# Projections of the linear attention and of the spatial gating given as units between the steps of the long convolutions

## The chip, the core and the metric

The kernel runs on one core of a Trainium2 chip. A core has five engines with a queue each: TensorE (PE; matmuls, with weight loads shown apart as PEld), VectorE (DVE), ScalarE (ACT), GpSimd (POOL) and SyncE (SP), which issues all DMA transfers of this kernel. The metric is the device time of one execution in microseconds (us).

## The reference, cut to what matters

One trunk layer is computed for 256 context tokens and 1024 latent tokens of width 1024. The input is normalised and modulated to `h`; one projection feeds four token mixers side by side, whose outputs are merged by `w_out`; a SwiGLU feed-forward block follows.

```python
h = rmsnorm(x, lp['g_pre1']) * (1.0 + sc1) + sh1
p = h @ lp['w_in']
ya = short_conv_mixer(p[..., :o1], lp['conv_a'], row_w)
yb, s_new = gla_mixer(p[..., o1:o2], s0, ...)       # linear attention
yc = chunk_mlp_mixer(p[..., o2:o3], ...)            # spatial gating
yd = hyena_mixer(p[..., o3:], ...)                  # long convolutions
m = jnp.concatenate([ya, yb, yc, yd], axis=-1) @ lp['w_out']
```

The long convolutions (`hyena_mixer`) gate a sequence twice with a bidirectional convolution as long as the sequence, by Fourier transforms. They need only their own columns of `p`. The linear attention needs its queries, keys, values, gates and decays, the spatial gating its two halves, all of them further columns of `p`.

## The kernel before

Everything is float32, and each product is made of three matmuls of split operands (`mm3`, lines 90 to 92): a high part and a remainder of each side. `hh` and `hl` hold the two parts of the transposed `h` for three column blocks of 512, 512 and 256 tokens (`CH`). `load_split` loads a weight (SyncE), casts it to its high part (ScalarE, line 65) and subtracts for the remainder (mostly DVE, line 66), in the seven tiles of pool `s4`.

A projection is cut into units. `proj_fm` makes 128 feature rows for one block: 24 matmuls of 512 or 256 columns into a PSUM bank (`pg`, four of them). `proj_rows` does so for three blocks, copies each with an activation on ScalarE and stores it to DRAM: three units to a weight. `proj_b` makes the linear attention's projections: gate rows with two weights (lines 866 and 867, six units) and then ten token tiles of 128 tokens by 288 columns (values and decays, 24 matmuls each; line 881 transposes the decays, line 883 copies them). `proj_c` makes the spatial gating's: two weights of feature rows (six units, copies on line 766) and ten token tiles of 256 columns (copies on line 778). These are 16 units each. `proj_c` is the beginning of the generator `fillers`, which goes on with the short convolutions (`mixer_a`) and the first tiles of `w_out`. `load_w` also steps the generator `later`, which loads the remaining modulation weights piece by piece and multiplies them (line 164).

`mixer_d` makes the long convolutions in 16 steps: two convolutions (`o`) of two channel tiles (`ct`), two halves (`q`) and two frequency tiles (`ft`). A step has a front (`hyena_front`: six matmuls of 320 columns from tiles `zh` and `zl` into a bank `p`, then scaling on ScalarE, lines 729 to 732, and combination on DVE, line 733, to a tile `Y`), and a back (`hyena_back`: butterflies and the product with the filter's spectrum `kk`, lines 705 to 751, on DVE, POOL and ScalarE). After every second step an inverse (`hyena_inverse`: twelve matmuls of 320 columns from `yh` and `yl`, lines 696 to 699) gives a half of the result. The back of a step is written behind the front of the next. At the end the results are transposed (lines 662 and 669), copied (665, 671, 672) and stored.

In `run`, `mixer_d` stands whole, then `proj_b` whole, then 17 steps of `fillers` (the 16 units of `proj_c` and the first of `mixer_a`), then `mixer_b`, the linear attention, which takes further units of `fillers` at marked places. The queries and keys are projected inside `mixer_b` by `proj_rows`.

The order of the code is not the order on the engines. The layer that builds the program puts the instructions on each engine's queue by priority, earlier code first, among those that it expects to be ready at that point, with tiles, banks and semaphores to be had. An engine then executes its queue in order. `tc.high_priority` and `tc.issue_after` bend that order in a few places.

Of the kernel before, what the change touches and what calls it, by code (L numbers as in the profile page):

```python
# [13 lines left out]
AF = mybir.ActivationFunctionType  # L14
# [4 lines left out]
P = 128  # L19
# [22 lines left out]
class Builder:  # L42
# [193 lines left out]
    def run(self):  # L236
        tc, nc, a = self.tc, self.nc, self.a
        with ExitStack() as ctx:
# [83 lines left out]
                    self.filter_spectra(flk, h2)  # L322
            rows = self.proj_d(w)
            with tc.tile_pool(name="psd", bufs=2, space=PSUM, reuse_waits="tile") as psd, sub("dm", side="right") as dm:
                self.mixer_d(dm, psd)
            self.proj_b(rows)
            self.wo, self.act1 = {}, (self.hh, self.hl)
            fill = self.fillers()
            for _ in range(17):
                next(fill)  # L330
            with banks() as self.psm, sub("bm", side="right") as bmx:
                self.mixer_b(bmx, fill)
            for _ in fill:
# [287 lines left out]
        xg = self.xg[kind][ct]  # L621
        nc.sync.dma_start(xg[:, n, 0:4, :] if n < 2 else xg[:, :, 4, :], sg[:, :N].rearrange("p (d c) -> p d c", c=P))

    def mixer_d(self, dm, psd):
        nc = self.nc
        self.p2 = lambda: psd.tile([P, 2, 512], F32, tag="p2", name=self.nm("p2"))
        self.hyena_consts(dm)
        zs = []
        for ct in range(2):
            z = dm.tile([P, 2, 5, P], F32, tag="z", bufs=3, name=self.nm("z"))  # L630
            nc.sync.dma_start(z, self.xg[0][ct])
            zs.append(z)
        back, done = None, []
        for o in range(2):
            for ct in range(2):
                z, gate = zs[ct], dm.tile([P, 2, 5, P], F32, tag="gate", bufs=1, name=self.nm("gate"))
                nc.sync.dma_start(gate, self.xg[o + 1][ct])
                zs[ct] = dm.tile([P, 2, 5, P], F32, tag="z", bufs=3, name=self.nm("z"))
                for q in (slice(0, 64), slice(64, 128)):
                    zq = self.hyena_split(dm, z[:, :, :, q])  # L640
                    ys = []
                    for ft in range(2):
                        kk = dm.tile([P, 5, 2, 64], F32, tag="kk", bufs=3, name=self.nm("kk"))
                        nc.sync.dma_start(kk, self.kd[o][ft][:, ct, :, :, q])
                        X = self.hyena_front(dm, ft, *zq)
                        if done:
                            self.hyena_inverse(dm, *done.pop())
                        if back:
                            back()

                        def back(X=X, ft=ft, ys=ys, kk=kk, gate=gate[:, :, :, q], dst=zs[ct][:, :, :, q]):
                            ys.append(self.hyena_back(dm, X, kk, ft))
                            if ft:
                                done.append((ys, gate, dst))
        back()
        self.hyena_inverse(dm, *done.pop())
        for ct in range(2):
            y2 = zs[ct]
            for kt in range(2):
                pt = self.p2()[:, 0]  # L660
                for p in range(4):
                    nc.tensor.transpose(pt[:, p * P:(p + 1) * P], y2[:, kt, p, :], self.ident)
                sg = dm.tile([P, 512], F32, tag="W", bufs=2, name=self.nm("dy"))
                pv = pt.rearrange("c (p u) -> c p u", p=4)
                nc.scalar.copy(sg.rearrange("c (u p) -> c p u", p=4), pv[:, :, ::-1] if kt else pv)
                nc.sync.dma_start(self.yd[6 + ct][:, kt * 512:(kt + 1) * 512], sg)
            pt = self.p2()[:, 0]
            for kt in range(2):
                nc.tensor.transpose(pt[:, kt * P:(kt + 1) * P], y2[:, kt, 4, :], self.ident)
            sg = dm.tile([P, 512], F32, tag="W", bufs=2, name=self.nm("dy"))  # L670
            nc.scalar.copy(sg[:, :P], pt[:, :P])
            nc.scalar.copy(sg[:, P:256], pt[:, 255:127:-1])
            nc.sync.dma_start(self.yd[6 + ct][:, 1024:1280], sg[:, :256])
# [46 lines left out]
    def hyena_front(self, dm, ft, zh, zl):  # L720

        nc = self.nc
        X = dm.tile([P, 5, 2, 64], F32, tag="Y", bufs=5, name=self.nm("Y"))
        t = dm.tile([P, 3, 2, 64], F32, tag="dt", bufs=2, name=self.nm("dt"))
        ps = self.p2()[:, :, :320].rearrange("p r (a c) -> p r a c", c=64)
        for ri in range(2):
            m = ri ^ ft
            self.mm3(ps[:, ri], self.dh[:, 0, ri, ft], self.dl[:, 0, ri, ft], zh[:, m], zl[:, m], True, True)
        nc.scalar.copy(X[:, ::4].rearrange("p a r c -> p r a c"), ps[:, :, ::4])
        for d in range(1, 4):  # L730
            nc.scalar.mul(t[:, d - 1, 0], ps[:, 1, d], self.twist(ft, d, 2))
            nc.scalar.mul(t[:, d - 1, 1], ps[:, 0, d], self.twist(ft, d, 1))
            nc.vector.scalar_tensor_tensor(X[:, d], ps[:, :, d], self.twist(ft, d, 0), t[:, d - 1], ALU.mult, ALU.add)
        return X

# [126 lines left out]

    def proj_b(self, rows):
        nc, a = self.nc, self.a
        self.proj_rows(rows, self.gd[0], AF.Silu)
        self.proj_rows(self.load_w(11), self.gd[1], AF.Silu)
        wv = []
        for k0, k1 in ((0, 3), (3, 6), (6, 8)):
            wv.append(self.load_split(a["wvg"][:, k0:k1, :].rearrange("p k c -> p (k c)"), (k1 - k0) * 288))
        for n, (n0, N) in enumerate(CH):  # L870
            pt = self.pg()
            for t in range(N // P):
                ps = self.pg()
                for kt in range(KT):
                    wh, wl = (x[:, (kt % 3) * 288:(kt % 3 + 1) * 288] for x in wv[kt // 3])
                    tk = slice(t * P, (t + 1) * P)
                    self.mm3(ps[:, :288], self.hh[n][:, kt, tk], self.hl[n][:, kt, tk], wh, wl, kt == 0, kt == KT - 1)
                o = self.pj()
                nc.scalar.copy(o[:, :288], ps[:, :288])
                nc.sync.dma_start(self.vd[:, n0 // P + t, :], o[:, :256])  # L880
                nc.tensor.transpose(pt[:, t * P:(t + 1) * P], o[:, 160:288], self.ident)
            o = self.pj()
            nc.scalar.copy(o[:, :N], pt[:, :N])
            nc.sync.dma_start(self.gkd[:, n0:n0 + N], o[:, :N])

    def proj_rows(self, w, dst, func, scale=1.0):
        nc = self.nc
        for n, (n0, N) in enumerate(CH):
            ps = self.proj_fm(w, n)
            o = self.pj()  # L890
            nc.scalar.activation(o[:, :N], ps[:, :N], func, scale=scale)
            nc.sync.dma_start(dst[:, n0:n0 + N], o[:, :N])

    def mixer_b(self, bm, fill):
        nc, a = self.nc, self.a
# [54 lines left out]
        cb = [x.rearrange("p (c t) -> p c t", t=P) for x in b]  # L950
        last = [cb[0][:, :, P - 1:P], cb[1][:, :, 0:1]]

        self.proj_rows(self.load_w(8), self.qd, AF.Identity, 32.0 ** -0.5)
        self.proj_rows(self.load_w(9), self.kkd, AF.Identity)

        def update(n, d):

# [51 lines left out]
        N, levels = 256, LEVELS + [0]  # L1009
# [760 lines left out]
```

## Time and profile before

| | |
|---|---|
| time, median of 3 runs | 1596.38 us (1595.15 to 1596.7) |
| profiled execution: time / span | 1599.48 us / 1597.70 us |
| mean granted TensorE clock | 0.976 of full speed |
| busy over the span: PE, PEld, DVE, ACT, POOL | 94%, 78%, 64%, 42%, 25% |
| instructions | 23281 |

The profile is of one execution. A busy figure is the time in which the engine had an instruction of its own running; matmuls are pipelined, so that a PE that is busy throughout may still run slower than it can, and the distance between the starts of two matmuls tells more than the length of one. Idle time is put down to the semaphore event that ended it.

### The profile page before, as it was taken

The numbers are of one execution on the slowest core, as the hardware profiler recorded it, in microseconds if no ns is written. First come the engines' busy times: TensorE is split into PE (matmuls) and PEld (weight loads), VectorE is DVE, ScalarE is ACT, GpSimd is POOL, SyncE is SP. The second block draws the span as 40 slices with busy tenths as digits, with TensorE's granted clock in tenths as the row PEclk, the third lists the DMA queues.
The fourth block names the chain that finished last, engine by engine and source line by source line (L and its number), as shares of the span: only waits on it lengthen the run. The fifth ranks groups of instructions, "written<-read, shape, count | busy, mean of one in ns | idle before, by whom it ended". The sixth has DMA issues, their size and how long they took to land.

```text
span 1597.7 us, 23281 instructions
## 1 busy us (share of the span) xinstructions
PE 1500.9 (94%) x8517; PEld 1239.1 (78%) x8517; DVE 1027.7 (64%) x1752; ACT 666.6 (42%) x1218; POOL 405.0 (25%) x406
## 2 busy tenths in 40 slices
PE   5999997888989889999899999999999999999996
PEld 2688877778668667788688888888888887888885
DVE  6776559999277898546746555665565635544467
ACT  5754245454356767555522222222222214433352
POOL 1433216556124665533211010101101000000004
PEclk9899999999999999999899999999999999999998
DMA  9335473442723074561134334443343428755576
GB/s 330 130 117 163 133 225 84 137 141 71 259 98 101 29 254 139 179 217 53 60 117 137 111 119 149 128 140 117 113 144 126 150 89 257 237 172 178 164 247 250
DMA packets 163226, 242.17 MB, mean 152 GB/s; under 512 B 34613, under 2 KB 97407, under 8 KB 162984
## 3 DMA queue, kind: packets, MB, share of 16 engines
q1 hardware_dynamic: 163112, 240.69, 46.2%
q8 instruction: 67, 1.10, 0.3%
q14 instruction: 47, 0.39, 0.1%
HBM read 169.05 MB, written 71.58 MB: 151 GB/s over the span
## 4 chain that ended last, share of the span: by engine, by line
PE 57%; DVE 8%; issue 3%; ACT 3%; DMA 2%; POOL 2%; SPq 0%; POOLq 0%; DVEq 0%; ACTq 0%
PE pg L1386 17%; PE pm L1386 7%; PE pg L1548 7%; PE pm L1548 6%; PE pg L92 4%; PE pg L90 4%; PE pg L91 3%; PE pm L90 3%; PE pm L92 3%; PE pm L91 3%; DMA raw<-w2t 1%; DVE qbd L1036 1%; POOL rs L98 1%; DVE hl L66 1%; PE pm L1049 1%
## 5 line engine op out<-in xcount | busy, mean ns | idle before, releaser
L92 PE MATMUL pg<-hh,s 128*128 128x512 f32 (+1 forms) x432 | 154.9, 363 | 6.7 <-DVE s L66 6.7
L90 PE MATMUL pg<-hh,s 128*128 128x512 f32 (+1 forms) x432 | 157.6, 366 | 3.7 <-ACT s L65 3.1
L66 DVE TENSOR_TENSOR op<-raw,op 128x1152 fp32r<-128x1152 f32 x69 | 93.7, 1357 | 100.6 <-ACT op L65 100.6
L91 PE MATMUL pg<-hl,s 128*128 128x512 f32 (+1 forms) x432 | 155.2, 360 | 0.6 <-POOL hl L204 0.6
L65 ACT CAST op<-raw 128x1152 fp32r<-128x1152 f32 x69 | 80.1, 1161 | 135.0 <-PE pg L1548 65.1
L1363 POOL TENSOR_TENSOR sr<-s,s 128x512 f32<-128x512 f32 x20 | 25.8, 1292 | 434.4 <-DVE sr L1361 434.4
L98 POOL TENSOR_TENSOR rs<-rs,mhalf 128x1 f32<-128x1 f32 x40 | 31.8, 798 | 354.7 <-DVE rs L97 351.4
L65 ACT CAST s<-s 128x1024 fp32r<-128x1024 f32 (+2 forms) x67 | 69.6, 1039 | 116.1 <-DMA s<-in_w 77.0
L1548 PE MATMUL pg<-op,op 128*128 128x512 f32 x372 | 115.3, 392 | 1.8 <-DVE op L66 1.8
L65 ACT CAST su<-sr 128x512 fp32r<-128x512 f32 x80 | 49.4, 620 | 149.6 <-PE pm L1386 59.7
L66 DVE TENSOR_TENSOR s<-s,s 128x1024 fp32r<-128x1024 f32 (+2 forms) x67 | 85.6, 1278 | 37.3 <-ACT s L65 20.6
L1386 PE MATMUL pg<-b1h,s 128*128 128x512 f32 x320 | 106.9, 395 | 0.7 <-ACT t L1393 0.7
L1386 PE MATMUL pg<-hh,su 128*128 128x512 f32 x320 | 107.3, 396 | 0.0
L1548 PE MATMUL pm<-op,op 128*128 128x512 f32 x338 | 104.5, 391 | 0.0
L90 PE MATMUL pm<-hh,s 128*128 128x256 f32 x352 | 100.0, 284 | 1.3 <-DVE tmp L201 1.3
L92 PE MATMUL pm<-hh,s 128*128 128x256 f32 x352 | 99.9, 284 | 0.0
L91 PE MATMUL pm<-hl,s 128*128 128x256 f32 x352 | 99.9, 284 | 0.0
L92 PEld LDWEIGHTS pg<-hh,s 128*128 128x128 f32 x432 | 82.5, 191 | 20.6 <-DVE s L66 7.6
L90 PEld LDWEIGHTS pg<-hh,s 128*128 128x128 f32 x432 | 82.5, 191 | 19.6 <-ACT s L65 4.5
L91 PEld LDWEIGHTS pg<-hl,s 128*128 128x128 f32 x432 | 82.5, 191 | 12.6 <-POOL hl L204 0.9
L1391 DVE TENSOR_TENSOR t<-t,pg 128x512 f32<-128x512 f32 x60 | 41.2, 687 | 77.9 <-PE pg L1386 71.5
L1548 PEld LDWEIGHTS pg<-op,op 128*128 128x128 f32 x372 | 70.2, 189 | 16.9 <-DVE op L66 2.3
(399 smaller groups left out, 4163.0 us busy)
## 6 DMA issues: line engine op xcount, KB each, us to landing
s<-in_wmod SPq DMA_DIRECT2D x48, 512.0 KB, 5.3
raw<-actd SPq DMA_DIRECT2D x75, 320.0 KB, 3.7
s<-in_w SPq DMA_DIRECT2D x44, 512.0 KB, 3.8
actd<-t SPq DMA_DIRECT2D x60, 256.0 KB, 3.7
tmp<-in_w SPq DMA_DIRECT2D x44, 256.0 KB, 3.2
w2t<-tmp SPq DMA_DIRECT2D x44, 256.0 KB, 2.1
raw<-w2t SPq DMA_DIRECT2D x44, 256.0 KB
s<-in_wfm SPq DMA_DIRECT2D x18, 512.0 KB, 5.0
```

The costliest lines, as they stand in the source:

```text
L65: nc.scalar.copy(hi, src)
L66: self.cut = (eng or nc.vector).tensor_tensor(lo, src, hi.bitcast(F32), ALU.subtract).ins
L90: mm(ps, lh, rh, start=start, stop=False)
L91: mm(ps, lh, rl, start=False, stop=False)
L92: self.last = mm(ps, ll, rh, start=False, stop=stop).ins
L98: nc.gpsimd.tensor_tensor(out, out, self.mhalf[:, :cols], ALU.pow)
L1036: (nc.scalar.copy if h > 1 else nc.vector.tensor_copy)(qb[hs, h, :], e[hs, 0])
L1049: nc.tensor.matmul(ps[32 * r:32 * r + 32, ci * 4 * wide:(ci + 1) * 4 * wide], kk[:, c * P + 32 * r:c * P + 32 * r + 32], qb[:, :, i0:i0 + ...
L1363: pt(s3, a1[:, c], a2[:, c], ALU.subtract)
L1386: self.last = mm(ps, l[:, k], r[:, k], start=start and k == 0 and i == 0, stop=stop and k == 3 and i == 2, skip_group_check=True).ins
L1391: add = lambda out, x, y: nc.vector.tensor_tensor(out, x, y, ALU.add)
L1548: mm(ps, l, r, start=start and i == 0, stop=stop and i == 2, skip_group_check=True)
```

## The change

`proj_b` and `proj_rows` become generators that yield after each unit. The 32 units of `proj_b` and `proj_c` are handed to `mixer_d`, which takes one behind each front and one behind each back: two in each of its 16 steps, which is all of them. One step of `fillers` remains behind `mixer_d` (the first unit of `mixer_a`). The queries and keys in `mixer_b` run through as before. No instruction is added, dropped or given other operands; what changes is the place in the code, and with that the priority, of the 32 units, their weight loads and the steps of `later` in these.

```diff
             with tc.tile_pool(name="psd", bufs=2, space=PSUM, reuse_waits="tile") as psd, sub("dm", side="right") as dm:
-                self.mixer_d(dm, psd)
-            self.proj_b(rows)
+                fill = itertools.chain(self.proj_b(rows), self.fillers())
+                self.mixer_d(dm, psd, fill)
+            for _ in range(1):
+                next(fill)
             self.wo, self.act1 = {}, (self.hh, self.hl)
-            fill = self.fillers()
-            for _ in range(17):
-                next(fill)
             with banks() as self.psm, sub("bm", side="right") as bmx:
                 self.mixer_b(bmx, fill)
...
-    def mixer_d(self, dm, psd):
+    def mixer_d(self, dm, psd, fill):
...
                         X = self.hyena_front(dm, ft, *zq)
+                        next(fill)
                         if done:
                             self.hyena_inverse(dm, *done.pop())
                         if back:
                             back()
+                        next(fill)
...
     def proj_b(self, rows):
         nc, a = self.nc, self.a
-        self.proj_rows(rows, self.gd[0], AF.Silu)
-        self.proj_rows(self.load_w(11), self.gd[1], AF.Silu)
+        yield from self.proj_rows(rows, self.gd[0], AF.Silu)
+        yield from self.proj_rows(self.load_w(11), self.gd[1], AF.Silu)
...
                 nc.tensor.transpose(pt[:, t * P:(t + 1) * P], o[:, 160:288], self.ident)
+                if t < N // P - 1:
+                    yield
             o = self.pj()
             nc.scalar.copy(o[:, :N], pt[:, :N])
             nc.sync.dma_start(self.gkd[:, n0:n0 + N], o[:, :N])
+            yield
...
             nc.scalar.activation(o[:, :N], ps[:, :N], func, scale=scale)
             nc.sync.dma_start(dst[:, n0:n0 + N], o[:, :N])
+            yield
...
-        self.proj_rows(self.load_w(8), self.qd, AF.Identity, 32.0 ** -0.5)
-        self.proj_rows(self.load_w(9), self.kkd, AF.Identity)
+        for _ in self.proj_rows(self.load_w(8), self.qd, AF.Identity, 32.0 ** -0.5):
+            pass
+        for _ in self.proj_rows(self.load_w(9), self.kkd, AF.Identity):
+            pass
```

## Rows read from the trace of the kernel before

**Rows 1.** The page: the span, and busy time, share of the span and instructions of TensorE (PE) and VectorE (DVE).

```profile
span 1597.7 us, 23281 instructions
...
PE 1500.9 (94%) x8517; PEld 1239.1 (78%) x8517; DVE 1027.7 (64%) x1752; ACT 666.6 (42%) x1218; POOL 405.0 (25%) x406
```

**Rows 2.** Busy time of each engine in five stretches. Columns: from:to and length in us, then PE, PEld, DVE, ACT and POOL busy (number of instructions in brackets), the granted TensorE clock as a share of full speed, the busy share of the DMA engines, GB/s. 223 to 398 us: the steps of the long convolutions; 398 to 421: their last inverse, transposes and stores; 421 to 600: most of the gated linear attention.

```profile
223.00:302.00 79.00, 67.04 (x429) 61.49 (x427) 71.20 (x148) 38.41 (x126) 45.77 (x34) 0.96 0.33 94
302.00:398.00 96.00, 82.92 (x515) 75.36 (x516) 89.83 (x195) 50.31 (x156) 57.38 (x43) 0.93 0.39 123
398.00:421.00 23.00, 20.89 (x117) 12.98 (x116) 7.55 (x14) 10.35 (x20) 7.71 (x9) 0.93 0.69 223
421.00:480.00 59.00, 51.92 (x263) 39.71 (x266) 31.48 (x64) 25.95 (x39) 11.02 (x14) 0.97 0.46 155
480.00:600.00 120.00, 107.85 (x1102) 86.86 (x1092) 105.96 (x217) 78.73 (x168) 71.36 (x99) 0.96 0.40 130
```

**Rows 3.** PE's instructions from 220 to 420 us by line and form, those of the projections that the change moves (line 90, the first of the three matmuls of a step; lines 91 and 92 have as many): output and input tiles, shape, number | busy us, mean ns | idle time of PE before them and what ended it.

```profile
L90 PE MATMUL pg<-hh,s 128*128 128x512 f32 x64 | 25.8, 404 | 1.8 <-ACT s L65 1.8
...
L90 PE MATMUL pg<-s,hh 128*128 128x288 f32 x80 | 25.6, 320 | 0.0
...
L90 PE MATMUL pg<-s,hh 128*128 128x256 f32 x80 | 23.1, 289 | 0.0
...
L90 PE MATMUL pg<-hh,s 128*128 128x256 f32 x32 | 9.0, 282 | 0.0
```

**Rows 4.** Who waited for whom, PE from 220 to 420 us, and the first line of the same for SyncE's DMA queue (SPq) from 223 to 421: line that waited, engine, tile and line waited for, us in total, times, longest us.

```profile
PE p L90 <- DVE Y L733: 10.7, 8, 2.7
PE p L90 <- ACT yh L65: 6.7, 4, 2.3
PE p L90 <- DVE z L698: 2.9, 2, 1.5
...
PE pg L90 <- ACT s L65: 1.8, 2, 1.2
PE pg L92 <- DVE s L66: 1.5, 1, 1.5
PE p L91 <- POOL yl L66: 1.0, 2, 0.6
...
SPq L644 <- DVE Y L742: 51.6, 12, 8.4
```

**Rows 5.** The view of one source line, for lines 742, 751 and 733, all on DVE: number; shortest, median and longest ns; first and last start.

```profile
L742 DVE TENSOR_TENSOR Y<-Y,kk x16: 812/818/1932, 233.0 to 394.8; 128x640 f32<-128x640 f32 x16
...
L751 DVE SCALAR_TENSOR_TENSOR Y<-Y,tw,dt x48: 334/350/1668, 241.5 to 403.7; 128x128 f32<-128x128 f32 x48
...
L733 DVE SCALAR_TENSOR_TENSOR Y<-p,tw,dt x48: 334/340/353, 225.8 to 389.5; 128x128 f32<-128x128 f32 x48
```

**Rows 6.** PE in order of time (start us, us, line, tiles, shape): two pairs of matmuls from which the spacing inside a unit is read, of a 512-column unit (239.77 to 241.13, six spacings) and of 256-column token tiles (361.75 to 362.94, ten); the first and the last matmul of front 9; the first of front 15.

```profile
239.77 0.39 PE L91 MATMUL pg<-hl,s 128*128 128x512 f32 x1
...
241.13 0.39 PE L91 MATMUL pg<-hl,s 128*128 128x512 f32 x1
...
361.75 0.28 PE L90 MATMUL pg<-s,hh 128*128 128x256 f32 x1
...
362.94 0.29 PE L91 MATMUL pg<-s,hh 128*128 128x256 f32 x1
...
312.41 0.40 PE L90 MATMUL p<-zh,dft_hi 128*128 128x320 f32 x1
...
313.23 0.31 PE L92 MATMUL p<-zh,dft_lo 128*128 128x320 f32 x1
...
381.31 0.31 PE L90 MATMUL p<-zh,dft_hi 128*128 128x320 f32 x1
```

**Rows 7.** The copies of the 288-column token tiles' gate rows (line 883) and of the gating's rows (line 766) on ScalarE, in the view of one source line (first and last start at the end of the figures); and, on DVE in order of time, the first run of line 733 for front 9.

```profile
L883 ACT COPY pj<-pg x3: 382/562/584, 278.5 to 315.0; 128x512 f32<-128x512 f32 x2, 128x256 f32<-128x256 f32 x1
...
L766 ACT ACTIVATE pj<-pg x6: 384/584/602, 322.2 to 358.7; 128x512 f32<-128x512 f32 x4, 128x256 f32<-128x256 f32 x2
...
319.61 0.34 DVE L733 SCALAR_TENSOR_TENSOR Y<-p,tw,dt 128x128 f32<-128x128 f32 x1
```

**Rows 8.** PE's instructions by line and form from 382.3 us (just behind front 15) to 412 us, the third matmul of the steps of the 256-column token tiles; and the view of line 778, the copies of these tiles on ScalarE.

```profile
L92 PE MATMUL pg<-s,hl 128*128 128x256 f32 x38 | 10.7, 282 | 0.0
...
L778 ACT ACTIVATE pj<-pg x10: 362/381/385, 365.2 to 403.5; 128x256 f32<-128x256 f32 x10
```

**Rows 9.** The tail in order of time: DVE's last product, PE with the transposes and what stands just ahead of them, SyncE's first load of the next stage from what the moved units stored.

```profile
410.59 0.82 DVE L699 TENSOR_TENSOR z<-z,gate 128x640 f32<-128x640 f32 x1
...
414.95 1.06 PE L164 MATMUL pg<-s,csil 128*32 128x512 f32 x8
415.94 1.09 PE L662 MATMUL p<-ident_sb,z 128*128 128x128 f32 x8
...
422.73 0.43 SPq L909 DMA_DIRECT2D gk<-gkd  x1
```

**Rows 10.** DVE's instructions from 223 to 412 us by line: number | busy us, mean ns | idle time before them and what ended it.

```profile
L751 DVE SCALAR_TENSOR_TENSOR Y<-Y,tw,dt 128x128 f32<-128x128 f32 x48 | 29.2, 625 | 1.5 <-ACT dt L750 1.4
...
L66 DVE TENSOR_TENSOR s<-s,s 128x1024 fp32r<-128x1024 f32 (+2 forms) x9 | 13.4, 1488 | 1.7 <-ACT s L65 1.7
```

**Rows 11.** The granted clock in a stretch of 4 us (columns as in rows 2).

```profile
308.00:312.00 4.00, 4.00 (x19) 4.00 (x18) 4.00 (x7) 1.70 (x4) 3.65 (x3) 0.51 0.45 94
```

## The prediction

> **What bounds the kernel now.** I read the page first: TensorE (PE) is busy 94% of a span of 1597.7 us and VectorE (DVE) 64% [rows 1]. That is an average over stages, so the second view is busy time by stage [rows 2]. While the long convolutions run (223 to 398 us), DVE is the full engine: 71.20 of 79 us, then 89.83 of 96. PE has 67.04 and 82.92. From 398 to 421 us, the tail of the convolutions, DVE has 7.55 of 23 us. The gated linear attention follows (421 to 600), with PE idle for 7.1 and 12.2 us.
>
> The third view, the form of each PE instruction, shows what PE does in the convolutions [rows 3]. Between 220 and 420 us it runs all the projections that the change moves: 80 steps each of the 288-column and 256-column token tiles, and 64 and 32 of the 512- and 256-column rows. So the units are **already there**, although the code stands behind the convolutions: each engine's queue is filled from what is expected to be ready, highest priority (earlier code) first, and the units are the fill. The change alters their priority against the convolutions, not the stage in which they run.
>
> The fourth view, who waited, tells what that costs [rows 4]. PE executes its queue in order. At the head of a convolution transform (tile p) it waited 10.7 us for line 733 to clear a bank, 6.7 us for the split of yh, 2.9 us for z and 1.0 us for yl, 21.3 us together, with units queued behind. The units themselves waited 3.3 us for the splits of their weights. The transforms stand too early in PE's queue for the DVE that there is.
>
> **The stage is paced by DVE.** Line 742, once in each of the 16 steps, runs at 233.0 first and 394.8 last: 10.8 us a step [rows 5]. PE needs less: a 512-column unit is 24 x 0.227 = 5.4 us, a 256-column rows unit and a 256-column token unit 24 x 0.12 = 2.9 us, a 288-column one, by its width, 3.2 us (spacing of starts in [rows 6]). The 32 units are 8 x 5.4 + 4 x 2.9 + 10 x 3.2 + 10 x 2.9 = 116 us, 7.2 us per step; transforms, a front of six 0.15 us matmuls in each step and an inverse of twelve in every second, add 1.8 us.
>
> **The change, part by part.** (1) *Which units move ahead of which front.* In the new order 2i units stand ahead of front i (counting from 0). Front 9 (312.41 us) comes before any of the spatial gating: the last copy of line 883 is at 315.0 and the first of line 766 at 322.2, so 16 units are ahead of it [rows 6, 7]. In the new order 18 are: two 512-column units, 10.9 us of PE work, move ahead. After front 15 (381.31) line 92 still runs 38 of its eight per 256-column token tile, 4.7 units; in the new order 2 [rows 6, 8]. So 2.7 units, 7.8 us, move ahead of the last front.
>
> (2) *What that removes.* Units placed ahead of a front fill the time in which PE now waits at its head. The 10.7 us of waits for line 733 cover 7.8 us at the last front, so this front should come no later, and PE should be through the 32 units about 7.8 us earlier.
>
> (3) *What that is worth.* While DVE sets the pace, nothing. It counts in the tail. There the last product of the convolution (line 699) ends at 411.41 us, and its transposes (line 662) start at 415.94, 4.5 us later: in PE's queue stand the rest of the first short-convolution unit and then eight modulation matmuls of line 164 [rows 9]. With that unit started 7.8 us earlier they go before the last inverse: **-4.5 us**. Copy, store and the first load of the attention (422.73) follow directly [rows 9], so that stage moves with them. The remaining 3.3 us of PE work land between 421 and 480 us, where PE idles for 7.1 us anyway: 0. Behind that PE is full, and what is ahead shifts one for one.
>
> (4) *What else moves.* Of each unit the copy on ScalarE and the store on SyncE move with it, of each weight the load, the cast and the subtraction (nine at 1488 ns on DVE, 13.4 us [rows 10]), and of each of the three moved weight-loading calls the modulation pieces that it steps. Their number is the same and all already run in this stage, so DVE's sum stays: 0. Their place is not shown by any row; bounds: a split moved ahead of convolution work delays one step by 1.5 us, or frees PE from the 3.3 us that units now wait for splits [rows 4]; I take 0, since both are DVE time that is spent either way. SyncE's queue is in order too: the loads of kk are held up to 8.4 us by buffers there [rows 4], but three buffers cover two steps of 10.8 us. If that cover were gone, a step would lose up to 8.4 us.
>
> (5) *The clock.* After its waits PE runs at a reduced granted clock: 0.51 from 308 to 312 us, practically the 1.2 GHz level, and 0.93 over 302 to 398 [rows 2, 11]. With fewer waits less of that; it is PE time in a stage that DVE sets, so 0, but it shortens the units and supports (2).
>
> **Sum.** The profiled execution took 1599.48 us, 1597.70 of it span; -4.5 gives 1595.0. Its time is 3.1 us above the median of the runs, 1596.38, from which I count: **1592 us**.
>
> **Rivals.** *Paced by DVE and Pool alone.* Line 751, whose tensors all lie in SBUF, takes 334 ns at least and 1668 at most, 625 on average; line 733, of the same shape but with one tensor in PSUM, never over 353, 340 in the median [rows 5, 10]. In 48 instructions that is 48 x 0.285 = 13.7 us of DVE time that only Pool, working beside it, explains, and no order of PE gives it back. In the tail the freed place in PE's queue is taken by the next fill (rows for the attention, a later unit), and the transposes stand behind that again: 0, so 1596.4. The forms in [rows 3] speak for it, the units being interleaved now, and that the change then does not really do what it says is part of this case; against it, the order at fronts 9 and 15 does change by 10.9 and 7.8 us. *The Trainium skill, "GPSIMD Engine Reference", section "1. Specifications", lists GpSimd's SBUF interfaces as shared with VectorE, with contention for DVE instructions that have two SBUF inputs. The rows agree; by that rule alone, rearranging PE in this stage gives 1596.4 us.*
>
> *Slower: fronts starve DVE.* At step 8 a front is followed by two 512-column units and an inverse: 0.9 + 10.9 + 1.8 = 13.6 us of PE against 10.8 of DVE. Front 9 now ends at 313.5 us; its first run of line 733 is at 319.61 [rows 6, 7]. If none of the waits before it is filled, it ends 10.9 us later, at 324.4, and line 733 starts at least 4.8 us later than now. DVE idles only 6.2 us from 302 to 398 [rows 2], so every such us goes to the end. It decides from the point where less than those 4.8 us of PE's idle time before front 9 (12.0 us in 223 to 302) are filled. Between 4.8 (front 9 alone) and 10.9 (no slack at all), middle 7: 1603 us. The same would follow if the copies of units, now ahead, held ScalarE's queue, in which the inputs of line 733 are made.
>
> *More than forecast.* The 7.8 us come fully on top, because PE and not a chain limits the attention: -12.3, 1584 us.
>
> **How the numbers follow.** A measurement of this kernel can tell about 0.2% (3.2 us) from no change. Chances: forecast, a gain of 3 to 9 us, 0.32; more than that 0.10; no effect 0.30; slower 0.28. The range runs from 1583 (the larger gain) to 1605 (the starved fronts near their upper bound); the forecast's own is 1588 to 1594. Faster 0.42, same 0.30, slower 0.28.
>
> **What would show it.** Right: PE's wait at p for line 733 falls from 10.7 us towards 3, the last copy of the gating's token tiles comes about 8 us before 403.5 [rows 8], the last transposes within 1 us of the last product, steps still 10.8 us. Wrong by the slower case: DVE idle between 302 and 398 rises above 10 us, with waits at line 733 for ScalarE, and steps 8 to 11 longer than 10.8. Wrong by the first rival: the same 4 us between last product and transposes. What would upset all of it is a different order of the attention stage behind, which I have taken as merely shifted.

## The result, and the profile after

The changed kernel takes 1609.93 us (median of 4 runs, 1608.92 to 1611.28) against 1596.54 us of the kernel before in the same comparison. The ratio is 1.0077, 95% interval 1.0062 to 1.0091: slower by 0.8%, some 12 us by the ratio and 13.4 by the two medians. The forecast was 1592 us, and the range ended at 1605.

Line numbers of the changed kernel are those of before plus 1 in the long convolutions (742 is now 743, 733 is 734, 662 is 663, 669 is 670), 767 and 779 for the gating's copies 766 and 778, 914 for the loads 909, 929 for the decays' matmuls (924), 981 for the attention's first update of its state (974). (In the kernel before, the two weights of the gate rows stand on lines 865 and 866.) The page: the same number of matmuls, busy on PE 2.8 us longer, on DVE 5.2 us longer [rows 1].

```profile
span 1609.5 us, 23264 instructions
PE 1503.7 (93%) x8517; PEld 1243.1 (77%) x8517; DVE 1032.9 (64%) x1752; ACT 663.7 (41%) x1218; POOL 403.4 (25%) x406
```

Busy time by stage of the changed kernel (columns as in rows 2, with one stretch more):

```profile
223.00:302.00 79.00, 68.80 (x429) 62.17 (x429) 73.53 (x144) 39.19 (x126) 43.09 (x34) 0.93 0.34 97
302.00:398.00 96.00, 86.05 (x540) 73.97 (x539) 89.51 (x190) 47.30 (x152) 54.26 (x41) 0.97 0.43 130
398.00:421.00 23.00, 20.29 (x102) 14.65 (x101) 13.66 (x23) 9.25 (x21) 10.90 (x10) 0.93 0.63 218
421.00:480.00 59.00, 49.34 (x233) 37.69 (x231) 22.63 (x48) 23.40 (x32) 4.65 (x8) 0.94 0.42 139
480.00:600.00 120.00, 104.79 (x1055) 85.82 (x1054) 102.42 (x225) 77.76 (x170) 72.39 (x102) 0.91 0.33 104
600.00:700.00 100.00, 89.02 (x591) 70.77 (x590) 69.06 (x139) 58.63 (x123) 52.33 (x63) 0.90 0.55 181
```

The kernel before from 600 to 700 us:

```profile
600.00:700.00 100.00, 93.99 (x602) 75.21 (x602) 63.51 (x136) 60.16 (x125) 45.43 (x60) 0.98 0.53 178
```

Read length less PE's busy time, row by row. In the convolutions (223 to 398) PE's idle time fell from 25.0 us [rows 2] to 20.2: the gain that the change was expected to make is there. From 398 to 700 us it rose from 27.4 to 38.6, and the granted clock fell from 0.96 and 0.98 to 0.91 and 0.90 in the last two rows. PE lost in the attention more than it had gained. (Part of the difference in the last two rows is only that the stage now lies 9 to 12 us further back.)

Who waited on PE, 220 to 420 us, in the changed kernel:

```profile
PE p L90 <- ACT yh L65: 6.4, 4, 3.1
...
PE p L90 <- DVE Y L734: 1.6, 1, 1.6
```

The 10.7 us of waits for line 733 [rows 4] are 1.6 now. The gating's last copy comes at 397.2 instead of 403.5 us [rows 8], but the last step's product comes at 399.5 instead of 394.8 [rows 5], which is 11.1 us a step where it was 10.8:

```profile
L743 DVE TENSOR_TENSOR Y<-Y,kk x16: 809/814/2247, 233.3 to 399.5; 128x640 f32<-128x640 f32 x16
```

```profile
L779 ACT ACTIVATE pj<-pg x10: 362/384/393, 350.3 to 397.2; 128x256 f32<-128x256 f32 x10
```

Behind the last front (front 15) only two of the gating's units are left (16 third matmuls, eight to a unit, where it was 38 [rows 8]; PE from 383.5 to 412 us):

```profile
L92 PE MATMUL pg<-s,hl 128*128 128x256 f32 x16 | 4.5, 282 | 0.0
```

At front 9 nothing of the kind happened. It starts at 307.97 instead of 312.41 us [rows 6], and the first of the gating's units starts just ahead of it and runs behind it:

```profile
307.40 0.50 PE L90 MATMUL pg<-hh,s 128*128 128x512 f32 x1
...
307.97 0.30 PE L90 MATMUL p<-zh,dft_hi 128*128 128x320 f32 x1
```

So PE was earlier and DVE later. Why DVE was later is in its instructions by line. First the kernel before, 223 to 421 us, four lines that were not shown, then the same of the changed kernel, 223 to 428 us:

```profile
L705 DVE TENSOR_TENSOR W<-Y 128x256 f32<-128x256 f32 x32 | 18.5, 592 | 2.4 <-POOL Y L745 2.0
...
L744 DVE TENSOR_TENSOR Y<-Y,Y 128x320 f32<-128x320 f32 x16 | 12.4, 777 | 4.9 <-POOL Y L743 4.9
...
L66 DVE TENSOR_TENSOR zl<-z,zh 128x320 fp32r<-128x320 f32 x7 | 4.7, 676 | 0.0
...
L66 DVE TENSOR_TENSOR zl<-zw,zh 128x320 fp32r<-128x320 f32 x7 | 3.9, 560 | 0.0
```

```profile
L752 DVE SCALAR_TENSOR_TENSOR Y<-Y,tw,dt 128x128 f32<-128x128 f32 x48 | 28.7, 621 | 2.8 <-ACT dt L751 2.8
L706 DVE TENSOR_TENSOR W<-Y 128x256 f32<-128x256 f32 x32 | 20.8, 669 | 0.7 <-POOL Y L746 0.5
L745 DVE TENSOR_TENSOR Y<-Y,Y 128x320 f32<-128x320 f32 x16 | 17.7, 1107 | 2.2 <-POOL Y L744 2.2
...
L66 DVE TENSOR_TENSOR zl<-z,zh 128x320 fp32r<-128x320 f32 x7 | 7.7, 1104 | 0.0
...
L66 DVE TENSOR_TENSOR zl<-zw,zh 128x320 fp32r<-128x320 f32 x7 | 5.8, 833 | 0.0
```

The same instructions in the same number take longer: 5.3 us more on line 745, 2.3 on 706, 3.0 and 1.9 on the two remainders zl. Over all lines of DVE in these two windows, with the few that got shorter, it is 8.1 us more, of which 1.9 are two products of the modulation (line 178) and 6.2 the convolutions and the splits. Line 752 shows no more contention than before (621 against 625 ns); others do. From the first product with kk to the last, DVE does 323 instructions in either kernel, is busy for 5.8 us more, and the stretch is 4.5 us longer, so the lateness is longer instructions and not waiting (before, then changed; columns as in rows 2):

```profile
233.00:394.79 161.79, 137.37 (x856) 126.36 (x854) 151.70 (x323) 81.72 (x258) 97.40 (x75) 0.94 0.37 110
```

```profile
233.30:399.55 166.25, 145.75 (x907) 128.15 (x905) 157.47 (x323) 81.92 (x261) 96.02 (x74) 0.95 0.39 116
```

For the remainders zl the two engines' timelines show what lengthened them (starts and ends on GpSimd are rough). Of the fourteen in the stage, three started while a GpSimd instruction was running before the change, and ten after it. Those that started otherwise took 0.48 or 0.49 us in either kernel, the others 0.48 to 1.84. One of the ten, with the GpSimd instruction beside it:

```profile
372.09 1.65 POOL L66 TENSOR_TENSOR yl<-Y,yh 128x640 fp32r<-128x640 f32 x1 [0.98 <-ACT yh L65]
...
372.24 1.84 DVE L66 TENSOR_TENSOR zl<-z,zh 128x320 fp32r<-128x320 f32 x1
```

The tail on DVE in order of time. In the second line a weight's remainder for the work behind, 2.56 us long, stands inside the last step of the convolutions.

```profile
399.55 0.82 DVE L743 TENSOR_TENSOR Y<-Y,kk 128x640 f32<-128x640 f32 x1
400.29 2.56 DVE L66 TENSOR_TENSOR s<-s,s 128x1024 fp32r<-128x1024 f32 x1
402.77 1.83 DVE L745 TENSOR_TENSOR Y<-Y,Y 128x320 f32<-128x320 f32 x1
...
415.87 0.82 DVE L700 TENSOR_TENSOR z<-z,gate 128x640 f32<-128x640 f32 x1
```

And on PE, behind that last product:

```profile
421.26 1.03 PE L663 MATMUL p<-ident_sb,z 128*128 128x128 f32 x8
422.05 0.48 PE L92 MATMUL pg<-hh,s 128*128 128x512 f32 x1
...
426.59 0.38 PE L670 MATMUL p<-ident_sb,z 128*128 128x128 f32 x2
```

From the end of the product (416.69) to its transposes are 4.6 us, as many as before (4.5, [rows 9]). The place that the short-convolution unit left in PE's queue was taken by rows for the attention's queries, and 20 more matmuls of these stand between lines 663 and 670.

SyncE's loads behind that, in the changed kernel:

```profile
430.73 0.42 SPq L914 DMA_DIRECT2D gk<-gkd  x1
...
436.96 0.59 SPq L914 DMA_DIRECT2D gk<-gkd  x1
437.65 10.50 SPq L83 DMA_DIRECT2D s<-in_wfm  x2
448.24 0.38 SPq L914 DMA_DIRECT2D gk<-gkd  x1
```

The first load of the attention is 8.0 us later than before (422.73, [rows 9]). The third stands behind two weight loads that wait for tiles of pool s4 (9.5 us, put down to a DMA into one and to line 66): 448.24 us. In the kernel before, the third load was issued at 436.76, just ahead of the same pair of weight loads (437.40, 13.48 us). The last matmul of the decays then comes at 457.1 us instead of 444.8, the first update of the state at 488.6 instead of 479.6, and the end is 11.8 us later.

### The profile page after: what moved, and what is told of

Same layout as the page of the kernel before. It is cut to its first block, busy times and chain, and to the rows that moved or that the text cites. A ratio compares the mean times of both kernels' runs of the same rounds, so it can differ in the third digit from the quotient of the medians.

```text
span 1609.5 us, 23264 instructions
## 1 busy us (share of the span) xinstructions
PE 1503.7 (93%) x8517; PEld 1243.1 (77%) x8517; DVE 1032.9 (64%) x1752; ACT 663.7 (41%) x1218; POOL 403.4 (25%) x406
## 4 chain that ended last, share of the span: by engine, by line
PE 67%; DVE 16%; issue 5%; ACT 5%; DMA 5%; POOL 2%; SPq 0%; DVEq 0%; POOLq 0%; ACTq 0%
PE pg L1393 17%; PE pg L1555 7%; PE pm L1393 7%; PE pm L1555 6%; PE pg L90 5%; PE pg L92 4%; PE pg L91 4%; PE pm L90 3%; PE pm L92 3%; PE pm L91 3%; DVE Y L752 1%; DVE hl L66 1%; DMA s<-in_wfm 1%; DVE Y L745 1%; DMA s<-in_wmod 1%
```

## The experiments

Two theories stood at first. **A:** DVE's instructions collide more with GpSimd's, so the convolutions end later, and the late tail then loses a place in SyncE's queue. **B:** the tail alone is at fault, where rows of the queries stand ahead of the last transposes. (The recorded expectations below use letters of their own, run by run.)

**The decay loads.** The rows of the decays are loaded into a tile of their own, unused until later (U), so that no load of theirs waits for a buffer behind weight loads. In the changed kernel and in the kernel before:

```diff
-            gk = load(bm.tile([P, 512], F32, tag="t", bufs=6, name=self.nm("gk")), self.gkd, n0, N)
+            gk = load(U.rearrange("p c d v -> p (c d v)")[:, n0:n0 + N], self.gkd, n0, N)
```

> The changed kernel, with the three loads of the decay rows (gkd) of the linear attention landing in a tile of their own (U, written only later), so that the second and third need not wait for a buffer and stand in SyncE's queue ahead of the weight loads. The steps of the convolutions keep their order. Theory A (the 13 us have two parts: the convolutions end 7 us later, and the third decay load, issued at 448.2 us instead of 436.8, stands behind a weight load that waits for a buffer, which makes 4 to 5 us more): 1602 to 1606 us, first exponential of the attention at 448 to 453 us instead of 459.3, last transposes unchanged at 426.6. Rival B (only the end of the convolutions counts, the load is covered): no change, 1608 to 1612. Rival C (the load is the whole loss): 1594 to 1599.

> The same edit in the kernel before, where the third decay load is issued at 436.8 us. Theory A: the loads gain up to 12 us there too, but the matmuls behind them stand in PE's queue among rows; 0 to 6 us faster than before, 1590 to 1597 us. If the edit brings as much here as in the changed kernel, the load explains nothing of the difference between the two.

Measured: 1603.78 us, ratio 1.0023 (1.0006 to 1.004), for the changed kernel with it; 1596.78 us, 0.9987 (0.9972 to 1.0002), for the kernel before. The three loads are issued together:

```profile
432.35 1.37 SPq L914 DMA_DIRECT2D U<-gkd  x3
```

So the change costs 0.36% where the third load can't be held, and 0.77% where it can: about half of the loss was that one place in SyncE's queue. The other half remains. In the changed kernel with this edit the first update still came late (485.4 us, in its twin 474.2), now behind the key rows, whose weight was late (PE, 420 to 500 us; the profiled execution, 1608.81 us, is the slowest of this run's ten):

```profile
PE pg L90 <- ACT s L65: 9.1, 1, 9.1
```

**The transposes first.** The changed kernel, with the short-convolution unit and the queries and keys ordered behind the last transposes:

```diff
-            for _ in range(1):
-                next(fill)
+            with tc.issue_after(self.lastT):
+                for _ in range(1):
+                    next(fill)
...
-                nc.tensor.transpose(pt[:, kt * P:(kt + 1) * P], y2[:, kt, 4, :], self.ident)
+                self.lastT = nc.tensor.transpose(pt[:, kt * P:(kt + 1) * P], y2[:, kt, 4, :], self.ident).ins
...
-        for _ in self.proj_rows(self.load_w(8), self.qd, AF.Identity, 32.0 ** -0.5):
-            pass
+        with self.tc.issue_after(self.lastT):
+            for _ in self.proj_rows(self.load_w(8), self.qd, AF.Identity, 32.0 ** -0.5):
+                pass
```

> The changed kernel, with PE's work on the next stage's rows (queries, keys, and the first unit of the short convolution) queued behind the last transposes of the long convolutions. Theory A: in the changed kernel 25 and 20 matmuls of 512 columns stand ahead of the last two groups of transposes (5.7 and 4.4 us); without them the last transposes come at 418 to 420 us instead of 426.6 and the time falls by 3 to 8 us, to 1602 to 1607. Rival B' (the lateness comes from DVE alone, PE's queue there is harmless): the transposes move by under 2 us and the time stays within 1608 to 1612, or rises as the rows come later.

> Both edits in the changed kernel. Theory A: what is left is DVE's later last step (399.5 against 394.8 us), about 5 us: 1598 to 1602 us. Rival: the two overlap and the sum is no better than the better of them.

Measured: 1615.39 us, 1.0104 (1.0085 to 1.0123), and with the decay edit too 1608.44 us, 1.0061 (1.004 to 1.0082). Neither is faster than its twin without that order; by the ratios they are 0.3 and 0.4% slower, with intervals that overlap or touch. The times that theory A of these two expectations gave (1602 to 1607 and 1598 to 1602 us) were missed. The last transposes did start earlier (419.7 us instead of 426.7), but PE stood still for them. Its busy time in the first of the two runs:

```profile
398.00:421.00 23.00, 10.83 (x40) 7.07 (x44) 11.78 (x22) 8.91 (x18) 10.78 (x10) 0.51 0.23 69
```

The attention needs decays and key rows, the first update came at 496.2 us (from 488.6), and **theory B found no support**: transposes that came 7 us earlier gained nothing. As the same order delayed the rows, these runs don't tell what earlier transposes alone would be worth.

**GpSimd out of the convolutions.** Lines 706, 743 and 745 (of before) and the remainder yl run on DVE instead, 80 instructions, in both kernels:

```diff
-        nc.gpsimd.tensor_tensor(w[:, 2:4], y[:, 0:2], y[:, 2:4], ALU.subtract)
+        nc.vector.tensor_tensor(w[:, 2:4], y[:, 0:2], y[:, 2:4], ALU.subtract)
...
-        nc.gpsimd.tensor_tensor(B, X, kb(1), ALU.mult)
+        nc.vector.tensor_tensor(B, X, kb(1), ALU.mult)
...
-        nc.gpsimd.tensor_tensor(A[:, :, 1], A[:, :, 1], B[:, :, 0], ALU.add)
+        nc.vector.tensor_tensor(A[:, :, 1], A[:, :, 1], B[:, :, 0], ALU.add)
...
-        self.split(A.rearrange(f), yh.rearrange(f), yl.rearrange(f), nc.gpsimd)
+        self.split(A.rearrange(f), yh.rearrange(f), yl.rearrange(f))
```

> The kernel before with the four kinds of GpSimd work in the long convolutions (lines 706, 743, 745 and the remainder of yh) given to VectorE. VectorE then has some 16 x 3 = 48 us more to do, but nothing beside it: a step of 11 to 12.5 us instead of 10.8, the last step's line 742 at 410 to 425 us, time 1605 to 1630. All instructions of one kind and place should then have the same length (line 751 at 340 to 360 ns on average instead of 625).

> The same in the changed kernel. Theory A (the 4.7 us by which the last step is late come from collisions of VectorE and GpSimd in SBUF, in which the same VectorE instructions took 199.1 instead of 191.0 us): without GpSimd the last line 742 / 743 starts within 1.5 us of that of the kernel before with the same edit. Rival B (the order of the queues: splits and copies of the units ahead of convolution work, fronts behind units): it stays 4 to 6 us later.

Measured: 1583.46 us, 0.9894 (0.9872 to 0.9917), for the kernel before with it; 1583.88 us, 0.9902 (0.9875 to 0.9929), for the changed one. The two are level (their intervals leave room for a difference of 0.3 to 0.4%), and both are 1% faster than the kernel before. The expectation that the steps would become longer was wrong: they are 10.0 and 9.9 us. DVE in the changed kernel with this edit, 223 to 421 us, by line, then the view of line 743 there:

```profile
L752 DVE SCALAR_TENSOR_TENSOR Y<-Y,tw,dt 128x128 f32<-128x128 f32 x48 | 15.4, 346 | 1.0 <-ACT dt L751 1.0
...
L706 DVE TENSOR_TENSOR W<-Y 128x256 f32<-128x256 f32 x32 | 13.4, 418 | 0.0
...
L745 DVE TENSOR_TENSOR Y<-Y,Y 128x320 f32<-128x320 f32 x16 | 7.7, 484 | 0.0
```

```profile
L743 DVE TENSOR_TENSOR Y<-Y,kk x16: 815/819/826, 231.3 to 379.5; 128x640 f32<-128x640 f32 x16
```

Line 752 takes 346 ns in the mean instead of 621, 706 takes 418 instead of 669, 745 takes 484 instead of 1107, and no line 743 is longer than 826 ns. The last step's product starts at 379.5 us, in the kernel before with this edit at 382.9 (its line 742): without GpSimd the new order is even 3.4 us ahead, more than the 1.5 us that theory A allowed. Of these, 1.3 us are there at the first product already. From the first product to the last, the stage takes 148.2 us in the new order and 150.3 in the old one without GpSimd. With GpSimd it took 161.8 to 162.3 us in three profiles of the old order (the kernel before, with the decay edit, with the weights early as below) and 166.1 to 166.4 in five of the new. The lateness of the changed kernel is therefore an effect of DVE and GpSimd working side by side. The edit takes away two things at once, the collisions and the hand-overs between the two engines; the means of the lines show the first, and how much the second adds stays open.

One thing spoke against a simple reading. The first update comes at 466.2 us in the changed kernel with this edit and at 477.7 in the kernel before with it, and yet both end together. Busy time of these two (the changed one first), 223 to 421 us, shows why:

```profile
223.00:302.00 79.00, 73.78 (x470) 67.31 (x469) 74.59 (x207) 44.39 (x143) 0.00 (x0) 0.94 0.43 132
302.00:398.00 96.00, 94.70 (x597) 78.77 (x596) 82.46 (x227) 52.89 (x153) 3.05 (x5) 0.98 0.47 150
398.00:421.00 23.00, 18.97 (x92) 12.85 (x90) 3.72 (x5) 5.39 (x11) 0.61 (x1) 0.85 0.68 234
```

```profile
223.00:302.00 79.00, 78.51 (x517) 72.46 (x516) 72.23 (x205) 45.95 (x141) 0.00 (x0) 1.00 0.47 143
302.00:398.00 96.00, 93.05 (x608) 77.02 (x607) 85.80 (x230) 52.94 (x158) 1.16 (x2) 1.00 0.51 163
398.00:421.00 23.00, 23.00 (x124) 19.94 (x123) 7.80 (x16) 7.12 (x11) 2.33 (x4) 1.00 0.42 134
```

Up to 421 us PE had been busy 187.5 us in the first and 194.6 in the second. What the second begins later in the attention it had done beforehand in other units. So the first update is a good sign of the end only between kernels that have done the same work by then.

**The weights of queries and keys early.** With the decay edit, the two weights are loaded ahead of the attention stage:

```diff
             self.wo, self.act1 = {}, (self.hh, self.hl)
+            self.wqk = [self.load_w(8), self.load_w(9)]
...
-        for _ in self.proj_rows(self.load_w(8), self.qd, AF.Identity, 32.0 ** -0.5):
+        for _ in self.proj_rows(self.wqk[0], self.qd, AF.Identity, 32.0 ** -0.5):
```

> The changed kernel with the decay rows landing in U, and the weights of queries and keys loaded ahead of the linear attention's constants instead of behind them. Theory A (behind the convolutions the first state update waits for the key rows; their weight's load stands in SyncE's queue behind a modulation piece and the attention's constants, which wait for the convolutions' buffers, so that a later end of the convolutions delays everything): key rows 5 to 10 us earlier than with the decay rows alone, time 1594 to 1600 us, level with the kernel before. Rival C (PE has this work to do in any order): no change against the decay rows alone, ratio 1.001 to 1.004 to before.

> The same two edits in the kernel before, where the weight of the keys is still loaded behind the attention's constants by the order of the queue. Theory A: little, as with the decay rows alone: ratio 0.996 to 1.000 to before.

Measured: 1595.88 us, 0.9987 (0.9972 to 1.0002), in the changed kernel; 1591.36 us, 0.9943 (0.992 to 0.9965), in the kernel before. The changed kernel becomes level with the kernel before, but its twin gains as much (0.0036 and 0.0044 beyond the decay edit; 0.996 to 1.000 was expected of the twin). A late key weight is thus a cost of both orders and **no cause of the difference**; that the first of these two came out level is a compensation, not an explanation.

**One unit in each step.** Only the linear attention's 16 units are given, one behind each front; the gating's stand behind the convolutions as before.

```diff
                         if back:
                             back()
-                        next(fill)
...
-            for _ in range(1):
+            for _ in range(17):
                 next(fill)
```

> The changed kernel with one unit in each of the 16 steps (behind the front), those of the linear attention's projections; the 16 of the spatial gating stand behind the convolutions again, as in the kernel before. In the first half of the convolutions the units then stand half as dense as in the changed kernel, in the second half their place is as before. If the loss grows with how far units move, about half of it: 1.002 to 1.005. If it arises in the second half of the stage and in the tail (gating weights and the next stage's weights against the last steps), level: 0.999 to 1.001, first update within 2 us of 479.6 us. If it arises at the beginning, where the linear attention's units come earlier, nearly the whole of it: 1.006 or more.

Measured: 1651.23 us, 1.0328 (1.0308 to 1.0347), far above what any of the three readings is about. Busy time from 302 to 398 us, and PE's modulation transposes in order of time:

```profile
302.00:398.00 96.00, 37.41 (x130) 30.51 (x130) 87.50 (x187) 43.89 (x144) 60.20 (x45) 0.57 0.25 74
```

```profile
400.80 1.05 PE L186 MATMUL pg<-ident_sb,tmp 128*128 128x128 f32 x4
```

PE is busy for 37 of 96 us at a clock of 0.57: no unit's matmuls run between 311 and 401 us. Line 186 is written with `issue_after(self.last)`, where `self.last` is the last matmul of the projections and transforms written so far. In the kernel before that is the last token tile of `proj_b`, here it is the last matmul of the last inverse, and the gating's units follow line 186. The next run sets `self.last` back to the token tile:

```diff
+            self.last = self.lastb
             for _ in range(17):
                 next(fill)
...
             nc.sync.dma_start(self.gkd[:, n0:n0 + N], o[:, :N])
+            self.lastb = self.last
```

> The kernel with one unit in each step again, but the modulation's transposes (line 186) are ordered behind the last token tile of the linear attention's projections, as the kernel before has it, instead of behind the last matmul written so far, which in the run before this one was that of the last inverse. If that order is what held the gating's units from 309 to 401 us and made 1.0328, they start near 315 us again and the time falls to 0.999 to 1.008, by how much the units of the first half matter: below 1.002 if the loss of the change arises in the second half and the tail, 1.004 or more if in the first half. If the gating's units were held by something else (their weights, buffers of their copies), the time stays above 1.02.

Measured: 1598.2 us, 1.0002 (0.999 to 1.0013): level. The transposes run early, and DVE's lines have about the means of the kernel before (745 at 818 ns, the remainder of z at 674, before 777 and 676):

```profile
311.32 0.60 PE L186 MATMUL pg<-ident_sb,tmp 128*128 128x128 f32 x4
```

But in this run the units hardly moved on the engines. The last gating copy is at 403.9 us, as before; front 9 starts at 311.68 us (before 312.41, changed 307.97); and PE's waits at the head of the fronts are still there (220 to 420 us):

```profile
PE p L90 <- DVE Y L734: 9.2, 7, 2.7
```

So the run shows that the place in the code costs nothing as long as the order on the engines stays. The loss came with two units in each step, where that order did change. Which of the moved units bring it is not shown.

**All three edits together**, in either kernel (diffs as above):

> The changed kernel with the three experimental edits together: no GpSimd work in the convolutions, the decay rows in a tile of their own, the query and key weights loaded ahead of the attention stage. If collisions and the late weight and decay loads are separate terms, the gains add: 0.9902 (GpSimd out) less some 0.010 (0.9987 against 1.0077, weights and decays early) gives 0.980 of the kernel before at best. If both edits pull the same thing forward (the first update of the attention, which came at 466.2 us with GpSimd out and at 477.9 us with the early weights, from 488.6), they don't add: 0.986 to 0.990, with the first update at 463 to 466 us. I expect the second, because with GpSimd out the update already comes 22 us earlier.

> The kernel before with the same three edits. GpSimd out alone gave 0.9894, the early weights and decays alone 0.9943. Added up they give 0.984; if they pull the same first update forward, 0.988. The order of the units is then the only difference to its twin; the theory of collisions and late loads says that no difference beyond 0.2% is left, either way. A theory that the new order helps once these two costs are gone would have the twin ahead by the 4.5 us of the forecast, 0.3%.

Measured: 1577.11 us, 0.9855 (0.9834 to 0.9877), in the changed kernel, and 1578.86 us, 0.9876 (0.9859 to 0.9893), in the kernel before. Both beat both kernels, by 1.2 to 1.5%. The first update came at 457.8 and 469.9 us. The gains don't add up fully. Between the two the intervals overlap: a remaining gain of the new order, 0.2%, is possible and not shown.

## Why the prediction was wrong

**Step 1 held at the last front and not at front 9.** Behind front 15 two units were left, as forecast. Ahead of front 9 there were still 16 units and not 18: the two units of 10.9 us did not move ahead of it, front 9 itself came 4.4 us earlier. **Step 2 held.** PE's waits for line 733 fell from 10.7 to 1.6 us, and the gating's units were through 6.3 us earlier (7.8 forecast). The steps, forecast at 10.8 us as before, took 11.1.

**Step 3, the -4.5 us, did not come.** Two of its parts failed. The gap between the last product and its transposes stayed (4.5, 4.6 us): the freed place in PE's queue was taken by the next fill, just as the first rival had said. And the product itself came 5.3 us later (411.41 to 416.69): 0.3 us at the first step, 4.5 over the steps, 0.5 in the last one.

**Step 4 is the step that failed.** It put the change in DVE's sum at 0, because no instruction is added. The number of instructions stayed and their length did not: 8.1 us more, on lines whose tensors lie in SBUF. One remainder of 2.56 us stood in the last step, where the bound had been 1.5, though that step was only 0.5 us longer. GpSimd out of the stage, the lateness was gone. The prediction had the means to see it, since its first rival read line 751 as 13.7 us of contention, but took that as a constant: "no order of PE gives it back". An order of PE moves DVE's instructions against GpSimd's, and here the sum rose: ten of fourteen remainders zl began beside GpSimd, where it had been three. The Trainium skill, "GPSIMD Engine Reference", section "1. Specifications", which the first rival named, says that GpSimd shares its SBUF interfaces with VectorE, with contention for VectorE instructions that have two SBUF inputs. The runs agree (line 752 takes 621 ns in the mean beside GpSimd and 346 without it). For the lines other than zl, which pairs collide more in the new order was not traced.

Step 4 put SyncE's queue at 0 as well and looked only at the loads of kk. The loss there was in the stage behind: the third decay load behind two weight loads, worth about 0.4% by the pair of runs with a tile of its own.

**Step 5.** The clock rose from 302 to 398 us (0.93 to 0.97), as said. It fell from 223 to 302 us (0.96 to 0.93) and behind 480 us, where PE had more idle time.

**The sum** took the attention as merely shifted. The prediction named that as what would upset it all, and gave no case for it. 0.36% of the 0.77% remains without that order of loads; it is of the size of the 5.3 us by which the last product is late. How the latter turns into the former, and where some 3 us between the first update (9.0 us late) and the end (11.8) arise, is only read from the trace and not shown by a run.

**The rivals.** That fronts starve DVE, the slower rival, came nearest to the time (1603) by a wrong mechanism, so that this nearness is luck: the two units that it puts ahead of front 9 did not go there, DVE idled 6.5 us from 302 to 398, as before (6.2), and PE's waits got shorter. The first rival was right in the tail, and right that DVE and GpSimd contend, and wrong in its total, as it held that sum constant. The larger gain fell with the tail.

## What to carry to other kernels

Where two engines contend for the same memory, the sum of one's instructions is not a constant of the order: give it a bound on both sides, from the shortest and the mean duration of each line, even if no instruction is added. An engine that "helps" the bounding one can cost as much as it takes over, as GpSimd did here: compare the mean of the bounding engine's lines with their shortest, and try it without the helper. A unit that moves in the code takes along what refers to "the last one so far", and its early end is worth something only if the next stage's loads don't stand behind other waits in an in-order queue.

## What the runs showed of the hardware

Without GpSimd, DVE did 80 instructions more between 223 and 421 us (13.5 us of line 706, 13.1 of 743, 7.8 of 745, 13.1 of yl, 47.5 in sum, by the kernel before with that edit) and was busy for 165.8 us, where it had been 168.6 [rows 2]. GpSimd's part of the work had cost DVE about as much as doing it. On GpSimd line 743 took 1606 to 3314 ns (the first run with one unit in each step):

```profile
L743 POOL TENSOR_TENSOR Y<-Y,kk x16: 1606/2256/3314, 228.5 to 388.2; 128x640 f32<-128x640 f32 x16
```

On DVE, with GpSimd idle, it takes 816 to 829 ns (the kernel before with that edit):

```profile
L743 DVE TENSOR_TENSOR Y<-Y,kk x16: 816/821/829, 233.3 to 383.6; 128x640 f32<-128x640 f32 x16
```

In the first run with one unit in each step, the second half of the convolutions (302 to 398 us) went through on a PE that was granted 0.57 of its clock and was busy for 37 of 96 us. From the first product to the last the stage took 156.7 us (230.0 to 386.7) instead of 161.8: PE does not set the pace there, DVE with GpSimd does. How much of the 5.1 us comes from the gating's copies and splits, part of which had left the stage too, is not shown.
